# First mixer: the substitution chain of the second pair of heads moved from VectorE to GpSimd

## The chip, the cores and the metric

The kernel runs on one core of a Trainium2 chip. The metric is the device time of one execution in microseconds, as the median of several runs. TensorE is called PE here, VectorE DVE, ScalarE ACT, GpSimd POOL or GpSimd; SP is the engine that issues most DMAs.

## The reference, cut to what matters

The network has a first block (a mixer of windowed attention and an RWKV-7 recurrence, then a gated feed-forward) and a second one of two layers. Sequence 512, width 1024, fp32. The change lies in the recurrence of the first mixer, 8 heads of 64:

```python
def step(state, inp):
    r_t, w_t, k_t, v_t, kk_t, a_t = inp
    sa = jnp.einsum('bhvk,bhk->bhv', state, -kk_t)
    state = (state * w_t[:, :, None, :]
             + sa[..., None] * (kk_t * a_t)[:, :, None, :]
             + v_t[..., None] * k_t[:, :, None, :])
    return state, jnp.einsum('bhvk,bhk->bhv', state, r_t)
```

## The kernel before, in words

Activations are kept with channels on the 128 partitions and the 512 positions along the row. Each dense product with a weight is done as three fp32r matmuls (L243 to L245), from an activation split in two parts (hh, hl) and a weight split in two (wh by ACT at L449, wl by DVE at L450). Weights come by DMA in pieces of 512 KB, through three buffers `raw` (L421, queue of SP).

The recurrence is done in chunks of 64 positions, for a pair of heads j (0 to 3) at a time. Its stages are written in the order that the string `order` in `CFG` gives (L21): D projects r, k and v; A makes decays and the small products within a chunk; I (`inverse_rows`) and J (`inverse_join`) invert a unit lower triangular matrix for each chunk and head; B runs over the eight chunk states. S is windowed attention for a group of heads, Q its query projection. A scheduler then places the instructions of every engine by dependences, priorities and its own estimates of durations, and each engine runs its list in order; the stages I are given a higher priority (L997).

`inverse_rows(j)` works on the two 32 x 32 halves of the diagonal of each 64 x 64 matrix, for 8 chunk-and-head units on the rows:

- L767: ACT fills T (`invt`, one buffer) with the identity; L771: DVE transposes the products `aab` into M (`invm`).
- L773 to L778: forward substitution, 31 steps of two instructions, each a chain link of the last:

```python
        for s in range(31):
            a, t = s // 4 + 1, 31 - s
            tv = tmp[:, :a * t].rearrange("p (a t) -> p a t", t=t)
            E("inv", j).tensor_tensor(tv, T[:, :a, s:s + 1].to_broadcast([P, a, t]),
                                    M[:, s + 1:, s:s + 1].rearrange("p t o -> p o t").to_broadcast([P, a, t]), op=OP.mult)
            E("inv", j).tensor_tensor(T[:, :a, s + 1:], T[:, :a, s + 1:], tv, op=OP.add)
```

- L780: four DMAs write T to DRAM (`s`); L782: GpSimd clears `RT`; L784: four DMAs read it back as diagonal blocks of `RT`.

`E(name, j)` picks the engine from `CFG[name][j]`: V is DVE, G GpSimd, A ACT. `inverse_join(j)` begins with two DVE transposes of RT into `rq` (L798), then matmuls of 32 x 32 (L803, L813). `stage_b(j)` applies RT (L833), adds to the queries (L848) and copies into F (L852), then goes through the states ST: L871 multiplies F with the last state on PE, L875 and L877 add the chunk's own products, L886 makes the next state on DVE (L884 for the first), L888 applies a state to the output. L881 clears the first state of a pair on GpSimd. `swa(j)` has score matmuls L935, softmax pieces L936 to L942, L950 transposes, L959 to L965 the row sums (L963 a reciprocal on DVE, L965 a wide copy of it on GpSimd), L970 values, L974 transposes of that copy, and L919 fetches bias rows by DMAs of GpSimd.

The numbers behind tile names are those of the buffers: `invt_1090`, `invp_1095` (the temporary) and `invm_1089` belong to the second pair, j = 1, `RT_1162` and `rq_1837` to its join; `ST_1304` to `ST_1359` are the states of the first pair.

Of the kernel before, what the change touches and what calls it, by code (L numbers as in the profile page):

```python
# [17 lines left out]
PSUM = bass.MemoryType.PSUM  # L18
DRAM = bass.MemoryType.DRAM

CFG = {'order': 'D0 PK A0 D1 Q0 Q1 I0 A1 I1 J0 B0 Q2 S0 Q3 D2 A2 J1 I2 S1 B1 S2 J2 D3 s0 S3 A3 I3 r1 J3 s2 s1 B2 s3 B3 r0 r2 r3 F', 'inv': 'VVVV', 'rt': 'G', 'bt': 'G', 'bh': 'G', 'kh': 'G', 'kk': 'V', 't1': 'V', 'th': 'G', 'at': 'A', 'ti': 'A', 'sh': 'V', 'bb': 'bbbs', 'ob': 'nnnw', 'fa': 2, 'oa': 2, 'yc': [1, 1], 'xc': [1, 1], 'xa': ['GVGGGGVV', 'GVGGVGGV'], 'ev': 0, 'mb': 'qqb', 'fb': 'qqb', 'rc': 1, 'xm': [('ld', 'cs', 'th', 'dec')], 'xf': [('z', 'z', 'z', 'z')], 'mp': 'on', 'fp': 'os', 'rkv': 5, 'wo0': 0, 'wo1': 0, 'up': 0, 'wi': 0, 'spare': '', 'ahead': 'bno|a', 'hpi': 200, 'uact': 'A'}  # L21

P = 128
S = 512
# [42 lines left out]
class K:  # L67
# [200 lines left out]
    def ffn(self, x, h, up, down, cw, nf, chunks, act, done, bc=None, parts=((0, S),), mid=None, before=None, after=None):  # L268
        nc = self.nc
        if bc is None:  # L270
            self.ahead(up, h, CFG["fa"])
            bc = self.rstd(x)
# [187 lines left out]
def post_add(k, x, y, g, eps, cols, h, g2, i):  # L460
    nc = k.nc
    bc = k.inv_rms(y, eps, chains=CFG["yc"][i])

    def apply():
        for m in range(8):
            yc, xc = y[m], x[m][:, cols[0]:cols[1]]
            nc.vector.scalar_tensor_tensor(yc, yc, k.pv[:, g + m:g + m + 1], bc, op0=OP.mult, op1=OP.mult)
            (nc.vector if CFG["xa"][i][m] == "V" else nc.gpsimd).tensor_tensor(xc, xc, yc, op=OP.add)
            k.scale(x[m], h[m], k.pv[:, g2 + m:g2 + m + 1], cols)
# [4 lines left out]
def boundary(k, x, h, st, applies, banks, tags, post, more=None):  # L474
# [3 lines left out]
    for i, cols in enumerate(HALVES):  # L478
# [3 lines left out]
        if more:  # L482
            more(cols)
        heads.append(k.squares([t[:, c0:c1] for t in x], CFG["xc"][i], tags[i]))
    st.ready += qs
# [12 lines left out]
def first_block(k, I, ctx):  # L498
    with k.phase("m1", dict(M1, rkv=CFG["rkv"])), k.tc.tile_pool(name="ps1", bufs=1, space=PSUM) as k.p1:
        x, h, up, bc = first_mixer(k, I)  # L500
    ps2 = ctx.enter_context(k.tc.tile_pool(name="ps2", bufs=1, space=PSUM))
    k.pairs = [ps2.tile([P, 2, S], F32, name=f"s{i}") for i in range(PAIRS)]
    for m in range(8):
        k.dump(f"x1_{m}", x[m])
    nc = k.nc
    k.c = ctx.enter_context(k.tc.tile_pool(name="cst2", bufs=1))
    with k.phase("f1", F1):
        y, applies, nxt, carry = [], [], [], []

        def done(m, q, acc, cols):  # L510
            nc.vector.tensor_tensor(acc, acc, q, op=OP.add)
            if cols == HALVES[0]:
                y.append([acc])
            else:
                y[m].append(acc)

        def mid():
            rope_tables(k, I, "z")
            carry.append(gate_weights(k, I))

        def before(i):
            if i == 1:
                nxt.append(k.stream(I["ev_w_in"]))
                nxt[1].pool = CFG["ev"]
                nxt[1].prepare(CFG["xf"])

        def after(i, cols):
            if i == 0:
                nxt.append(k.scaled_tiles())
            applies.append(post_add(k, x, [t[i] for t in y], PV["n_ffn_post"], 1e-6, cols, nxt[0], PV["attn_n0"], i))  # L530

        down = k.stream(I["w_ffn_down"])
        k.ffn(x, h, up, down, PV["cw1"], act=AF.Gelu_apprx_tanh, done=done, bc=bc, parts=HALVES, mid=mid, before=before, after=after, **FFN1)
        h, st = nxt
        q = k.pss()
        bc = boundary(k, x, h, st, applies, CFG["fb"], ("zu", "u"), CFG["fp"], lambda cols: gate_dense(k, q, carry[0], h, cols))
    for m in range(8):
        k.dump(f"x2_{m}", x[m])
    return x, h, st, bc, q
# [1336 lines left out]
```

## Time and profile before

| | us |
|---|---|
| median of 3 runs | 2214.72 |
| lowest and highest | 2212.98, 2216.64 |
| profiled execution, its own time | 2216.11 |
| its span in the trace | 2214.4 |

The span is what the views divide; the 1.7 us between it and the execution's own time lie outside the trace. In a timeline each row has the start, the duration, the engine, the line of the kernel, operation, output and inputs without buffer numbers, and in brackets how long the engine sat idle before it and what ended that. [...]

### The profile page before, as it was taken

What the parts mean: (1) busy time and instruction counts of PE and PEld (TensorE: products, weight loads), DVE (VectorE), ACT (ScalarE), POOL (GpSimd) and SP (SyncE); (2) the same over time, 40 slices, a digit from 0 to 9 for tenths busy, and PEclk for the clock granted to TensorE, in tenths of its full rate; (3) what the DMA queues carried; (4) which work ended last, traced back from release to release, by engine and by line L of the source; (5) the groups of instructions that cost most, each with busy time, mean ns of one, the idle gap of its engine ahead of it and who ended that gap; (6) DMA issues with size and microseconds to landing.
All of it is one profiled execution on the core that took longest, in us unless ns stands there. A gap on an engine that the chain in (4) does not pass through costs nothing. (4 is left out here: it accounts for less than half of the span.)

```text
span 2214.4 us, 30032 instructions
## 1 busy us (share of the span) xinstructions
PE 2134.9 (96%) x11732; PEld 1707.0 (77%) x11736; DVE 1388.4 (63%) x2478; ACT 920.7 (42%) x1519; POOL 354.1 (16%) x331
## 2 busy tenths in 40 slices
PE   7899988999999999999999999999999899999998
PEld 6676767888888889976777888888666568888887
DVE  5988856767246666544676653664795656644665
ACT  4345534544234444333444432443334444433443
POOL 2111105111001113201102111111013201111111
PEclk9999998999999999999999999999999999999999
DMA  4210131333323335311112233332211113333334
GB/s 159 72 43 25 54 96 39 91 98 104 98 95 95 99 130 170 110 60 46 57 58 86 95 97 98 100 96 95 68 58 58 38 39 95 96 95 95 98 121 153
DMA packets 66301, 192.81 MB, mean 87 GB/s; under 512 B 15808, under 2 KB 19152, under 8 KB 66160
## 3 DMA queue, kind: packets, MB, share of 16 engines
q1 hardware_dynamic: 65584, 189.70, 27.1%
q0 software_dynamic: 576, 1.19, 0.3%
q8 instruction: 92, 1.51, 0.3%
q14 instruction: 49, 0.40, 0.1%
HBM read 188.24 MB, written 2.63 MB: 86 GB/s over the span
## 5 line engine op out<-in xcount | busy, mean ns | idle before, releaser
L450 DVE TENSOR_TENSOR wl<-raw,wh 128x1024 fp32r<-128x1024 f32 x341 | 431.8, 1267 | 259.9 <-ACT wh L449 259.3
L243 PE MATMUL q<-hh,wh 128*128 128x512 f32 (+1 forms) x1294 | 518.8, 401 | 12.1 <-ACT hh L210 7.7
L449 ACT ACTIVATE wh<-raw 128x1024 fp32r<-128x1024 f32 x341 | 359.8, 1056 | 371.1 <-PE q L244 207.2
L244 PE MATMUL q<-hl,wh 128*128 128x512 f32 (+1 forms) x1294 | 507.2, 392 | 3.8 <-DVE hl L211 3.8
L245 PE MATMUL q<-hh,wl 128*128 128x512 f32 (+1 forms) x1294 | 505.2, 390 | 0.2 <-DVE wl L450 0.2
L243 PEld LDWEIGHTS q<-hh,wh 128*128 128x128 f32 x1294 | 246.4, 191 | 61.8 <-ACT hh L210 7.7
L244 PEld LDWEIGHTS q<-hl,wh 128*128 128x128 f32 x1294 | 246.6, 191 | 53.8 <-issue 6.0
L245 PEld LDWEIGHTS q<-hh,wl 128*128 128x128 f32 x1294 | 246.0, 190 | 52.8 <-issue 2.9
L243 PE MATMUL b<-hh,wh 128*128 128x512 f32 (+1 forms) x602 | 237.5, 394 | 0.0
L244 PE MATMUL b<-hl,wh 128*128 128x512 f32 (+1 forms) x602 | 231.6, 385 | 1.5 <-DVE hl L211 1.5
L245 PE MATMUL b<-hh,wl 128*128 128x512 f32 (+1 forms) x602 | 231.8, 385 | 0.0
L294 POOL TENSOR_TENSOR zu<-za,z 128x512 f32<-128x512 f32 x76 | 100.8, 1327 | 814.6 <-DVE z L289 758.6
L243 PE MATMUL q<-gh,wh 128*128 128x256 f32 (+1 forms) x559 | 189.2, 338 | 2.5 <-ACT wh L449 1.4
L245 PE MATMUL q<-gh,wl 128*128 128x256 f32 (+1 forms) x559 | 188.8, 338 | 1.2 <-DVE wl L450 1.1
L244 PE MATMUL q<-gl,wh 128*128 128x256 f32 (+1 forms) x559 | 187.7, 336 | 0.0
L150 ACT ACTIVATE gh<-zu 128x512 fp32r<-128x512 f32 x76 | 48.1, 632 | 250.5 <-POOL zu L294 250.5
L151 DVE TENSOR_TENSOR gl<-zu,gh 128x512 fp32r<-128x512 f32 x76 | 52.6, 692 | 150.8 <-ACT gh L150 150.8
L183 POOL TENSOR_TENSOR nsq<-nsq,nsq 128x256 f32<-128x256 f32 (+1 forms) x84 | 97.3, 1160 | 253.9 <-ACT nsq L178 253.6
L287 ACT ACTIVATE z<-u,pv 128x512 f32<-128x512 f32 x152 | 122.6, 809 | 31.2 <-DVE u L286 31.2
L244 PEld LDWEIGHTS b<-hl,wh 128*128 128x128 f32 x602 | 114.2, 190 | 24.1 <-DVE hl L211 2.3
L245 PEld LDWEIGHTS b<-hh,wl 128*128 128x128 f32 x602 | 114.0, 189 | 23.4 <-issue 1.0
L243 PEld LDWEIGHTS b<-hh,wh 128*128 128x128 f32 x602 | 114.3, 190 | 22.7 <-issue 2.7
(589 smaller groups left out, 3241.7 us busy)
## 6 DMA issues: line engine op xcount, KB each, us to landing
raw<-in_ffn_up SPq DMA_DIRECT2D x88, 512.0 KB, 3.4
raw<-in_w_ffn_up SPq DMA_DIRECT2D x64, 512.0 KB, 3.4
raw<-in_ffn_down SPq DMA_DIRECT2D x55, 512.0 KB, 3.4
raw<-in_w_ffn_down SPq DMA_DIRECT2D x48, 512.0 KB, 3.4
raw<-in_ev_w_in SPq DMA_DIRECT2D x24, 512.0 KB, 3.5
raw<-in_w_in SPq DMA_DIRECT2D x20, 512.0 KB, 3.5
raw<-in_od_w_in SPq DMA_DIRECT2D x20, 512.0 KB, 3.4
x<-in_x SPq DMA_DIRECT2D x16, 256.0 KB, 3.7
```

The lines of the kernel that those rows point to most:

```text
L150: nc.scalar.activation(hi, x, AF.Copy)
L151: nc.vector.tensor_tensor(lo, x, hi.bitcast(F32), op=OP.subtract)
L183: (nc.gpsimd if m % chains == 0 else nc.vector).tensor_tensor(acc, acc, sq, op=OP.add)
L243: nc.tensor.matmul(o, wh, xh, start=(k == 0), stop=False)
L244: nc.tensor.matmul(o, wh, xl, start=False, stop=False)
L245: nc.tensor.matmul(o, wl, xh, start=False, stop=(k == n - 1))
L287: nc.scalar.activation(y, v, AF.Identity, bias=col(3), scale=col(2))
L294: nc.gpsimd.tensor_tensor(u, a, z[1], op=OP.mult)
L449: nc.scalar.activation(a, part, AF.Copy)
L450: (nc.gpsimd if self.pool > 0 else nc.vector).tensor_tensor(b, part, a.bitcast(F32), op=OP.subtract)
```

## The change

One letter of `CFG` is changed, and with it the engine that the two instructions of a step run on for j = 1:

```diff
-CFG = {'order': '...', 'inv': 'VVVV', ...}
+CFG = {'order': '...', 'inv': 'VGVV', ...}
```

The 62 instructions of the second pair leave DVE's list and enter GpSimd's. The scheduler also places others anew around them. Three places:

GpSimd, between stage A of the second pair (`kk_930`, `th_925`) and the clearing of a first state; the chain's start, the changed order.

```order
L724 TENSOR_TENSOR kk_930<-kti_973,dec_927 128x512
L723 TENSOR_TENSOR th_925<-ksq_931,dec_927 128x512
L776 TENSOR_TENSOR invp_1095<-invt_1090,invm_1089 128x31
L778 TENSOR_TENSOR invt_1090<-invt_1090,invp_1095 128x31
L776 TENSOR_TENSOR invp_1095<-invt_1090,invm_1089 128x30
L778 TENSOR_TENSOR invt_1090<-invt_1090,invp_1095 128x30
```

Before, the second of these rows was followed by L782, the clearing of `RT_1162`; that now stands in the middle of the chain, and L881 (`ST_2143`) and L965 (`sws_1506`) behind its last row.

DVE, in the states of the first pair (ST) and the attention of the first group (es, sws); the order before, at the second pair's join.

```order
L644 TENSOR_TENSOR u_1588<-q_1557,bc_352 128x512
L450 TENSOR_TENSOR wl_1633<-raw_1630,wh_1632 128x1024
L647 SCALAR_TENSOR_TENSOR rkv_1590<-u_1588,pv,rkv_1590 128x511
L798 STREAM_TRANSPOSE rq_1837<-RT_1162 32x256 x2
L910 TENSOR_TENSOR rwo_1395<-rwo_1395,b_1398 128x512
```

And the changed order, where the two transposes stand now:

```order
L886 SCALAR_TENSOR_TENSOR ST_1332<-ST_1323,pc_558,b_1326 128x128
L938 TENSOR_REDUCE es_1441<-sws_1481 128x2
L798 STREAM_TRANSPOSE rq_1837<-RT_1162 32x256
L886 SCALAR_TENSOR_TENSOR ST_1341<-ST_1332,pc_558,b_1335 128x128
L939 TENSOR_TENSOR es_1441<-es_1441,nsink_414 128x2
L1094 SCALAR_TENSOR_TENSOR swq_1555<-q_1524,bc_352 128x512
L450 TENSOR_TENSOR wl_1597<-raw_1594,wh_1596 128x1024
L886 SCALAR_TENSOR_TENSOR ST_1350<-ST_1341,pc_558,b_1344 128x128
L959 TENSOR_TENSOR es_1441<-es_1441,sink_412 128x8
L798 STREAM_TRANSPOSE rq_1837<-RT_1162 32x256
```

The pair of transposes moved up from behind the third pair's first projection into the first pair's states, one ahead of ST_1341 and one behind ST_1350.

SP, the DMAs of the second pair's chain among the loads of w_in; the difference.

```order
 L421 DMA raw_2373<-in_w_in 128x1024
-L421 DMA raw_2409<-in_w_in 128x1024
 L780 DMA s_1_1088<-invt_1090 32x8x32 x4
 L784 DMA RT_1162<-s_1_1088 32x8x32 x4
+L421 DMA raw_2409<-in_w_in 128x1024
 L421 DMA raw_2445<-in_w_in 128x1024
```

One weight load moved behind the eight DMAs of the chain. On ACT, the filling of the third pair's T (L767, `invt_1881`) moved up, ahead of the weight copy `wh_1596` and the exponentials of `sws_1481`. On PE the instructions are the same; ahead of the matmul L871 that reads ST_1341 there are two fewer of the projections `q_1524` and `q_1557`.

## Rows read from the trace of the kernel before

**Rows 1.** The page, busy time of each engine over the whole span

```profile
PE 2134.9 (96%) x11732; PEld 1707.0 (77%) x11736; DVE 1388.4 (63%) x2478; ACT 920.7 (42%) x1519; POOL 354.1 (16%) x331
```

**Rows 2.** Windows around the chain: stretch, us, PE, PEld, DVE, ACT, POOL busy, PEclk

```profile
125.00:130.00 5.00, 5.00 (x63) 4.40 (x63) 4.55 (x20) 3.75 (x12) 0.00 (x0) 1.00 0.00 0
130.00:135.00 5.00, 3.77 (x115) 3.53 (x117) 4.45 (x19) 1.47 (x5) 0.95 (x1) 1.00 0.01 3
135.00:150.00 15.00, 14.87 (x145) 10.98 (x141) 12.63 (x48) 5.89 (x17) 1.57 (x4) 1.00 0.11 37
```

**Rows 3.** Waits of PE, 120 to 170 us: total, times, longest

```profile
PE b L843 <- ACT F L852: 1.2, 1, 1.2
```

**Rows 4.** Timeline of DVE: start, us; chain's transpose, a state step, chain's last

```profile
123.18 1.97 DVE L771 STREAM_TRANSPOSE invm<-aab 128x1024 f32<-128x1024 f32 x1 [0.38 <-ACT aab L770]
...
144.81 0.35 DVE L886 SCALAR_TENSOR_TENSOR ST<-ST,pc,b 128x128 f32<-128x128 f32 x1
...
151.11 0.16 DVE L778 TENSOR_TENSOR invt<-invt,invp 128x8 f32<-128x8 f32 x1
```

**Rows 5.** Timeline of DVE: the join's transposes and a later weight split

```profile
159.04 0.89 DVE L798 STREAM_TRANSPOSE rq<-RT 32x256 f32<-32x256 f32 x2
...
169.52 1.23 DVE L450 TENSOR_TENSOR wl<-raw,wh 128x1024 fp32r<-128x1024 f32 x1 [0.22 <-ACT wh L449]
```

**Rows 6.** Groups of GpSimd by shape, two-input products: busy us, mean ns of one

```profile
L294 POOL TENSOR_TENSOR zu<-za,z 128x512 f32<-128x512 f32 x76 | 100.8, 1327 | 814.6 <-DVE z L289 758.6 <-ACT za L292 50.6 <-DVE strictb L1045 5.4
...
L1567 POOL TENSOR_TENSOR e<-e,sg 128x127 f32<-128x127 f32 x8 | 3.1, 409 | 64.7 <-DVE sg L1566 64.7
```

**Rows 7.** Timeline of DVE, then of GpSimd: a release, and the clearing of RT

```profile
116.35 0.16 DVE L705 TENSOR_SCALAR ar<-kk 128x8 f32<-128x8 f32 x1
...
116.65 1.36 POOL L724 TENSOR_TENSOR kk<-kti,dec 128x512 f32<-128x512 f32 x1 [0.77 <-DVE ar L705]
...
130.11 0.95 POOL L782 MEMSET RT<- 128x1024 f32 x1 [11.08 <-PE b L833]
```

**Rows 8.** Groups of DVE by shape: chain's two operations, a 512-wide product

```profile
L776 DVE TENSOR_TENSOR invp<-invt,invm 128x60 f32<-128x60 f32 x12 | 3.2, 266 | 0.2
...
L714 DVE TENSOR_TENSOR kti<-rkv,ld 128x512 f32<-128x512 f32 x4 | 2.7, 683 | 0.0
...
L778 DVE TENSOR_TENSOR invt<-invt,invp 128x60 f32<-128x60 f32 x12 | 2.6, 217 | 0.2
```

**Rows 9.** Timeline of DVE, the first pair's chain: first, second, twentieth instruction

```profile
82.84 0.21 DVE L776 TENSOR_TENSOR invp<-invt,invm 128x31 f32<-128x31 f32 x1
83.08 0.19 DVE L778 TENSOR_TENSOR invt<-invt,invp 128x31 f32<-128x31 f32 x1
...
87.76 0.23 DVE L778 TENSOR_TENSOR invt<-invt,invp 128x66 f32<-128x66 f32 x1
```

**Rows 10.** Timeline of DVE, the fourth pair's chain: its end, the join's transpose

```profile
291.50 0.18 DVE L778 TENSOR_TENSOR invt<-invt,invp 128x8 f32<-128x8 f32 x1
...
295.72 0.43 DVE L798 STREAM_TRANSPOSE rq<-RT 32x256 f32<-32x256 f32 x1 [0.89 <-DMA RT<-s]
```

**Rows 11.** Timeline of PE: a state step, the transposes of attention

```profile
145.62 0.38 PE L871 MATMUL b<-ST,F 128*128 128x128 f32 x2
...
150.97 0.66 PE L974 MATMUL w<-ident,sws 128*128 128x128 f32 x4
```

**Rows 12.** Windows around two pauses of PE; columns as in rows 2

```profile
104.90:108.20 3.30, 0.01 (x1) 0.01 (x1) 3.30 (x10) 0.37 (x1) 2.42 (x2) 1.00 0.03 12
109.80:113.00 3.20, 3.20 (x8) 1.76 (x7) 2.41 (x4) 1.17 (x2) 0.00 (x0) 0.51 0.22 33
332.80:338.10 5.30, 5.30 (x24) 5.29 (x25) 2.65 (x6) 1.59 (x4) 1.46 (x2) 0.50 0.00 0
```

**Rows 13.** Timeline of SP, then of ACT: weight loads, T's initial copy

```profile
114.20 32.62 SPq L421 DMA_DIRECT2D raw<-in_w_in  x2
...
156.54 0.40 ACT L767 ACTIVATE invt<-tinit 128x256 f32<-128x256 f32 x1
```

More of the change, by code (lines that the diff above doesn't have):

```diff
@@ L19 @@
 DRAM = bass.MemoryType.DRAM
-CFG = {'order': 'D0 PK A0 D1 Q0 Q1 I0 A1 I1 J0 B0 Q2 S0 Q3 D2 A2 J1 I2 S1 B1 S2 J2 D3 s0 S3 A3 I3 r1 J3 s2 s1 B2 s3 B3 r0 r2 r3 F', 'inv': 'VVVV', 'rt': 'G', 'bt': 'G', 'bh': 'G', 'kh': 'G', 'kk': 'V', 't1': 'V', 'th': 'G', 'at': 'A', 'ti': 'A', 'sh': 'V', 'bb': 'bbbs', 'ob': 'nnnw', 'fa': 2, 'oa': 2, 'yc': [1, 1], 'xc': [1, 1], 'xa': ['GVGGGGVV', 'GVGGVGGV'], 'ev': 0, 'mb': 'qqb', 'fb': 'qqb', 'rc': 1, 'xm': [('ld', 'cs', 'th', 'dec')], 'xf': [('z', 'z', 'z', 'z')], 'mp': 'on', 'fp': 'os', 'rkv': 5, 'wo0': 0, 'wo1': 0, 'up': 0, 'wi': 0, 'spare': '', 'ahead': 'bno|a', 'hpi': 200, 'uact': 'A'}
+CFG = {'order': 'D0 PK A0 D1 Q0 Q1 I0 A1 I1 J0 B0 Q2 S0 Q3 D2 A2 J1 I2 S1 B1 S2 J2 D3 s0 S3 A3 I3 r1 J3 s2 s1 B2 s3 B3 r0 r2 r3 F', 'inv': 'VGVV', 'rt': 'G', 'bt': 'G', 'bh': 'G', 'kh': 'G', 'kk': 'V', 't1': 'V', 'th': 'G', 'at': 'A', 'ti': 'A', 'sh': 'V', 'bb': 'bbbs', 'ob': 'nnnw', 'fa': 2, 'oa': 2, 'yc': [1, 1], 'xc': [1, 1], 'xa': ['GVGGGGVV', 'GVGGVGGV'], 'ev': 0, 'mb': 'qqb', 'fb': 'qqb', 'rc': 1, 'xm': [('ld', 'cs', 'th', 'dec')], 'xf': [('z', 'z', 'z', 'z')], 'mp': 'on', 'fp': 'os', 'rkv': 5, 'wo0': 0, 'wo1': 0, 'up': 0, 'wi': 0, 'spare': '', 'ahead': 'bno|a', 'hpi': 200, 'uact': 'A'}
 P = 128
```

## The prediction

> **What bounds the kernel now.** First the page: TensorE (PE) is busy for 2134.9 of 2214.4 us [rows 1], so a change elsewhere counts only where it makes PE wait or ends a wait of PE. Then the windows around the chain that moves. PE is busy 5.00 of 5.00, 3.77 of 5.00 and 14.87 of 15.00 us there, while DVE carries the whole chain beside its other work [rows 2]. PE's list of waits from 120 to 170 us has one entry above 0.3 us: 1.2 us at L843, for ACT's copies into F, which waited for DVE's L848 [rows 3]. Then DVE's own timeline: the chain's source M is ready at 125.15 us (123.18 + 1.97), and its 62nd instruction ends at 151.27 (151.11 + 0.16) [rows 4]. Nothing on PE waits for it. The join, whose two transposes read what the chain leads to, runs at 159.04 [rows 5]. So the chain costs this kernel nearly nothing where it is: it is spread through 26 us in which PE has other work.
>
> **What the change removes.** 62 instructions leave DVE. At most PE gets back the 1.2 us at L843. I book nothing for it, because this wait lies ahead of a new one, told below, and what PE gains before a wait it loses in it. The remaining waits of PE there are shorter still.
>
> **What the chain takes on GpSimd.** The 62 instructions come in a row, each needing the one before. The 31 products (L776) work on 31, 30, 29, 28, 54, ... 16, 8 elements, 1560 in all, and the 31 additions (L778) on as many: 3120. No row shows GpSimd at such sizes; the nearest are its two-input products of 127 elements, 409 ns, and of 512, 1327 ns [rows 6]. A line through both is 918 / 385 = 2.38 ns an element and 106 ns an instruction. That gives 62 x 0.106 + 3120 x 0.00238 = 6.6 + 7.4 = 14.0 us. Between two dependent instructions lies a release. DVE's L705 ended at 116.51 and GpSimd's L724, which waited for it, began at 116.65: 0.14 us, so 62 x 0.14 = 8.7 us. RT's clearing, 0.95 us, stands in the middle of the chain in GpSimd's queue [rows 7]. The products read M with a stride; on DVE such a product takes 266 ns where the addition of the same size takes 217 [rows 8], and I give GpSimd the same 49 ns, 31 x 0.049 = 1.5 us. Sum T = 14.0 + 8.7 + 0.95 + 1.5 = 25.2 us.
>
> The bounds: at least 14.0 us with DVE's own 0.03 us between two instructions (83.05 to 83.08) [rows 9] and RT's clearing for nothing, 14.0 + 1.9 = 15.9 us. At most 62 x (0.409 + 0.14) + 0.95 = 35.0 us, if none is cheaper than the smallest that a row shows. I take 25.2, since the fitted line and the measured release are both rows of GpSimd.
>
> **Who waits for it.** The way back is the fourth pair's: its chain ends at 291.68 (291.50 + 0.18), and the join's first transpose, which sat idle for the DMA into RT, starts at 295.72 [rows 10]: 4.04 us for the way through DRAM. In the changed order this transpose stands on DVE ahead of the step that makes the fifth state, ST_1341, and DVE runs in order. So the chain's end now decides when this step runs: 4.04 + 0.43 (L798) + 0.35 (L886, 0.35 in [rows 4]) = 4.8 us behind it. Behind that DVE has the query's scaling, a weight split and the next state step; PE has, in order, L871 on ST_1341, then projections, attention and the rest. PE cannot pass.
>
> Before, PE began this L871 at 145.62 [rows 11]. The new order has two projection matmuls fewer ahead of it, 0.23 us each by their spacing, so the same point of work is 145.2. Now it can begin at 125.15 + T + 4.8 = 129.95 + T. The shift of everything behind is T - 15.25 us; for T = 25.2, **10.0 us**. The attention transposes L974 at 150.97 [rows 11], whose input GpSimd copies after the chain, do not wait again: that copy needs DVE's reciprocal, itself behind the late state step.
>
> **The clock.** [...] The new pause would be about 10 us, and I add **2.0 us**.
>
> **What costs nothing.** On SP the load of raw_2409 now stands behind the eight DMAs of this chain; it went out near 146.8, at the end of [rows 13]'s two loads, and goes now near 155. Its weights are split at 169.52 [rows 5], which leaves over 10 us; without that cover the cost would be the lateness itself. On ACT, T's refill for the third pair (L767, 0.40 us) moves from 156.54 [rows 13] to ahead of a weight copy, and waits until the chain's DMAs have read T. They are done before the RT transfers that follow them, so ACT is free before DVE is; its backlog up to the next exponentials is about 2 us, and PE first needs those about 1.5 us after it resumes. If that cover fails, it is half a microsecond. GpSimd's later work is now queued behind the chain, whose end I put at 150.4. L965 has to wait for a reciprocal that comes after the late state step anyhow, and the bias rows fetched behind it are first used two projections later. DVE work beside GpSimd's short instructions up to L798 mostly has PSUM as a source, and DVE would wait at L798 anyhow.
>
> **Sum.** 10.0 + 2.0 = 12.0 us. The profiled execution took 2216.11 us (span 2214.4), and would take 2228.1. The median of the runs, 2214.72, is 1.4 lower; against it I predict **2226.7 us**.
>
> **Rivals.**
> First, not slower: GpSimd works through its dependent instructions without the release of 0.14 us and cheaper than the line says, T up to 15.25 us. Then the transpose finds RT there in time, and what remains is up to 1.2 us regained: 2213.5 to 2214.7. The point at which it decides is T = 15.25, 246 ns for each instruction. For it: DVE manages such an instruction in about 0.25 us. Against it: the line alone gives 14.0 us, leaving 1.25 us for 62 releases and RT's clearing. Faster by more than 0.2% would take more than all PE waits of this stretch together.
>
> Second, GpSimd is to DVE at every size what it is at 512 elements: 1327 against 683 ns [rows 6, 8], a ratio of 1.94. DVE's chain by itself, 20 instructions from 82.84 to 87.99 without a break [rows 9], is 0.26 us each, 62 x 0.26 = 16.1 us. Times 1.94 plus 0.95 is T = 32.2, a shift of 17.0 and some 2.3 us for the clock: 2234. For it: both engines have fixed costs an instruction. Against it: at 127 elements the line shows no such fixed cost. [...]
>
> Third, the upper bound: no instruction below 409 + 140 ns, or DVE and GpSimd hinder each other at each one; T = 35.0, a shift of 19.75 and 2.65 for the clock: 2237.1. Nothing in the profile speaks for so high a floor but the lack of a smaller row.
>
> **How the numbers follow.** Forecast (T from 18 to 30, 2219 to 2232) 0.53; ratio 0.22; upper bound 0.10; not slower 0.15. A difference of 0.2%, 4.4 us, is about what a measurement of this kernel can tell from no change. The three slow cases hold 0.85, of which 0.01 falls short of 0.2%; the not-slower case gives 0.11 to no change and 0.04 to faster. So: faster 0.04, same 0.12, slower 0.84. The range must reach into the ends: low 2216, the lower bound T = 15.9 and a little of the clock; high 2238, just past the upper bound. It leaves out the not-slower case, 0.15, and little else.
>
> **What would show it.** In the changed profile: 62 GpSimd rows of L776 and L778 with about 0.4 us from start to start, the last ending near 150; a DVE row L798 with some 10 us of idle before it, released by the DMA into RT; a wait of PE of about that length at L871, released by DVE's L886; a stretch with the clock at 0.5 behind it; the same work later by 12 us from there to the end. It is wrong if the chain ends before 140.4, if L798 finds RT ready, or if PE's wait lies at another line.

## The result, and the profile after

| | us |
|---|---|
| kernel before, median of 4 runs beside the change | 2215.37 |
| changed kernel, median of 4 runs (lowest, highest) | 2228.52 (2226.57, 2230.05) |
| ratio, 95% interval | 1.0062, 1.0048 to 1.0075 |
| profiled execution, its own time; its span | 2228.38; 2226.4 |

The change makes the kernel slower, by 12.0 us in the spans of the two profiled executions (13.2 us by the medians). The medians of later sessions are told with those of the runs of the kernel before that went with them; in each session 4 to 6 of these lie between 2222 and 2227 us, some 10 us above the rest, and pull the ratio that goes with the interval down, so that a slower version looks less slow by the ratio than by the medians, and a faster one faster.

The page's first part. Against [rows 1] DVE lost 62 instructions and 10 us, GpSimd gained 62 and 18 us:

```profile
PE 2136.8 (96%) x11732; PEld 1707.4 (77%) x11736; DVE 1378.2 (62%) x2416; ACT 920.5 (41%) x1519; POOL 372.0 (17%) x393
```

The windows from 140 us on, columns as in [rows 2]; PEclk is the clock granted to PE, 1.00 its full speed. PE does nearly nothing for nine microseconds, and the granted clock stands at 0.50 when it goes on:

```profile
140.00:145.00 5.00, 5.00 (x45) 3.46 (x46) 1.99 (x4) 0.00 (x0) 4.00 (x13) 1.00 0.00 0
145.00:150.00 5.00, 0.56 (x3) 0.12 (x2) 0.00 (x0) 0.00 (x0) 3.50 (x14) 0.88 0.00 0
150.00:155.00 5.00, 0.60 (x2) 0.50 (x2) 1.31 (x5) 2.33 (x5) 0.00 (x0) 0.50 0.31 48
155.00:160.00 5.00, 5.00 (x30) 3.65 (x29) 2.25 (x7) 1.30 (x6) 0.20 (x1) 0.59 0.35 109
```

The list of PE's waits between 100 and 200 us now begins with the step that makes a state; the 1.2 us at L843 [rows 3] are 0.3:

```profile
PE b L871 <- DVE ST L886: 8.8, 1, 8.8
...
PE b L843 <- ACT F L852: 0.3, 1, 0.3
```

GpSimd's timeline: the chain's first three instructions, RT's clearing within it, and the last. From 125.75, when DVE's L771 ends (123.79 + 1.96, against 125.15 in [rows 4]), to 149.53 it takes 23.8 us:

```profile
125.83 0.26 POOL L776 TENSOR_TENSOR invp<-invt,invm 128x31 f32<-128x31 f32 x1 [6.19 <-DVE invm L771]
126.17 0.25 POOL L778 TENSOR_TENSOR invt<-invt,invp 128x31 f32<-128x31 f32 x1
126.50 0.25 POOL L776 TENSOR_TENSOR invp<-invt,invm 128x30 f32<-128x30 f32 x1
...
137.89 0.36 POOL L776 TENSOR_TENSOR invp<-invt,invm 128x75 f32<-128x75 f32 x1
138.18 0.96 POOL L782 MEMSET RT<- 128x1024 f32 x1
139.09 0.34 POOL L778 TENSOR_TENSOR invt<-invt,invp 128x75 f32<-128x75 f32 x1
...
149.32 0.21 POOL L778 TENSOR_TENSOR invt<-invt,invp 128x8 f32<-128x8 f32 x1
```

DVE's timeline. The last row before the gap ends at 143.52; then DVE stands at the join's first transpose until the DMA into RT has landed, and the state step that PE wants comes behind it:

```profile
142.84 0.68 DVE L938 TENSOR_REDUCE es<-sws 128x2 f32<-128x512 f32 x1
153.69 0.43 DVE L798 STREAM_TRANSPOSE rq<-RT 32x256 f32<-32x256 f32 x1 [10.17 <-DMA RT<-s]
154.06 0.29 DVE L886 SCALAR_TENSOR_TENSOR ST<-ST,pc,b 128x128 f32<-128x128 f32 x1
```

ACT's timeline shows a second queue that stands still for the same chain, 13.02 us at the refill of the single buffer T. It is let go when the chain's DMAs have read T, about 1 us before DVE:

```profile
152.66 0.42 ACT L767 ACTIVATE invt<-tinit 128x256 f32<-128x256 f32 x1 [13.02 <-DMA s<-invt]
152.98 1.04 ACT L449 ACTIVATE wh<-raw 128x1024 fp32r<-128x1024 f32 x1
153.93 0.58 ACT L951 ACTIVATE swt<-w 128x512 f32<-128x512 f32 x1
```

PE's timeline at the pause, and attention's transposes of [rows 11] behind it:

```profile
145.16 0.40 PE L243 MATMUL q<-hh,wh 128*128 128x512 f32 x1
154.40 0.79 PE L871 MATMUL b<-ST,F 128*128 128x128 f32 x2 [8.84 <-DVE ST L886]
...
162.43 0.66 PE L974 MATMUL w<-ident,sws 128*128 128x128 f32 x4
```

Where the 12.0 us are: this L871 comes 8.78 us later than in [rows 11] with two projections (0.46 us) still to do, so 9.2 us there, 8.84 of them the wait. L974 comes 11.46 us later; the 2.2 us between the two are the lower clock, 0.50 up to 155 us and 0.59 on average from 155 to 160. 0.5 us more are lost behind it.

One comparison reads against intuition: on DVE the chain ended at 151.27 [rows 4], on GpSimd at 149.53. GpSimd had it done sooner, having nothing but RT's clearing beside it in those 23.8 us. What changed for the worse is where the chain's readers stand.

### The profile page after: what moved, and what is told of

It is laid out like the page before. It is cut to its first block, busy times and chain, and to the rows that moved or that the text cites. A ratio compares the mean times of both kernels' runs of the same rounds, so it can differ in the third digit from the quotient of the medians.

```text
span 2226.4 us, 30038 instructions
## 1 busy us (share of the span) xinstructions
PE 2136.8 (96%) x11732; PEld 1707.4 (77%) x11736; DVE 1378.2 (62%) x2416; ACT 920.5 (41%) x1519; POOL 372.0 (17%) x393
```

## The experiments

The theory: two in-order queues, DVE's at L798 and ACT's at L767, were given the chain's readers ahead of work for PE, and either alone would hold PE nearly as long; the chain on GpSimd costs nothing by itself. The rivals are told with the runs.

**DVE's readers moved back.** The transposes are tied to a value that exists only after the third pair's first projection:

```diff
-        Rc = k.slot("rq", (P, 8, 32))
+        Rc = k.slot("rq", (P, 8, 32)); j == 1 and nc.vector.tensor_copy(Rc[:, 0, 0:1], DP[2][0][:, 0:1])
```

> The changed kernel with one thing undone: DVE's two join transposes of the second pair (L798) are tied to a value of the third pair's first projection, so that they stand on DVE behind L647 and L910, some 20 us later than in the changed kernel, where they stood before the change. The chain stays on GpSimd. Theory A, two queues wait side by side (DVE at L798, ACT at the refill of T, L767, single buffer): DVE's wait is gone, PE passes L871 near 145.5 us, but ACT still stands at L767 until about 152.7, then does a weight copy and two exponentials, so that PE waits at L950 from about 148 to 155.5; with the lower clock behind it about 2225 us (2222 to 2228). Theory B, only DVE's transpose holds PE: no wait above 1.5 us is left, 2214 to 2217. Theory C, the loss comes from GpSimd itself (its later queue, its traffic beside DVE, SP's delayed weight load): about 2228, PE's wait at another line than L871 and L950.

Measured: 2225.05 us against 2215.64 (ratio 1.0038, 1.0025 to 1.0051). PE's waits from 95 to 175 us, and ACT's timeline:

```profile
PE w L950 <- ACT swt L951: 7.4, 1, 7.4
```

```profile
152.50 0.42 ACT L767 ACTIVATE invt<-tinit 128x256 f32<-128x256 f32 x1 [13.02 <-DMA s<-invt]
...
154.75 0.57 ACT L951 ACTIVATE swt<-w 128x512 f32<-128x512 f32 x1
```

DVE's wait is gone and PE is held at another line, by ACT, from 148.0 to 155.4. That is theory A, in the line and the length of the wait; theories B and C fall.

**ACT's reader set free.** The second pair gets its own T:

```diff
-        M, T = k.slot("invm", (P, 32, 32)), k.slot("invt", (P, 8, 32))
+        M, T = k.slot("invm", (P, 32, 32)), k.slot("invu" if j == 1 else "invt", (P, 8, 32))
```

> The changed kernel with one thing undone: the second pair has a buffer of its own for T, so that ACT's refill of T for the third pair (L767) no longer waits for the second chain's DMAs. DVE's transposes stay where the change put them. Theory A and theory B: DVE's L798 still waits about 10 us, PE's wait at L871 stays at 8.5 to 9 us, ACT has no wait above 4 us; 2226 to 2229 us. Theory D, ACT's wait is what holds PE and DVE's only ends at the same time: PE's wait shrinks to under 3 us, below 2220.

Measured: 2227.45 us against 2215.64 (ratio 1.0039, 1.0024 to 1.0055). PE's waits, and ACT's longest:

```profile
PE b L871 <- DVE ST L886: 8.9, 1, 8.9
```

```profile
154.97 0.51 ACT L942 ACTIVATE sws<-sws,es 128x256 f32<-128x256 f32 x1 [8.80 <-DVE es L939]
```

PE's wait is as it was, and D falls. One point of the expectation was wrong: ACT does wait above 4 us, 8.80 us, now for DVE's L939, which stands behind L798 too.

**Both.** The two edits together.

> Both edits together, chain on GpSimd. Theory A: neither queue stands behind the chain any more; PE has no wait above 1.5 us between 120 and 170 us and keeps the full clock there; 2213 to 2216 us, the time of the kernel before. The chain itself still takes 23 to 25 us on GpSimd. Theory C (GpSimd's own later work, SP's weight load behind the chain's DMAs, or traffic of GpSimd beside DVE is part of the loss): between 2218 and 2228 us, with a wait of PE at a line behind these.

Measured: 2215.78 us against 2215.64 (ratio 0.9996, 0.9983 to 1.0008). The first rows of PE's waits from 95 to 175 us, and the windows in which PE stood still in the changed kernel:

```profile
PE o L718 <- DVE invt L778: 3.3, 1, 3.3
PE o L691 <- ACT ld L675: 0.8, 1, 0.8
```

```profile
145.00:150.00 5.00, 5.00 (x40) 3.25 (x39) 3.28 (x7) 1.00 (x3) 4.28 (x13) 1.00 0.00 1
150.00:155.00 5.00, 4.90 (x26) 3.69 (x22) 3.86 (x16) 1.32 (x3) 0.88 (x2) 1.00 0.52 95
```

The whole loss is gone, with the chain on GpSimd as in the changed kernel (124.29 to 149.11, 24.8 us). GpSimd's later work, SP's late weight load and traffic beside DVE cost nothing that a run can tell: theory C falls.

**The same edits on the kernel before.**

> Control: the kernel before, chain on DVE, with the same two edits (a buffer of its own for the second pair's T, the transposes tied behind the third pair's first projection). Theory A: the edits by themselves are worth nothing, 2213.5 to 2216.5 us, PE's 1.2 us at L843 is still there. If it comes out faster than that, the edits are worth something of their own, and the run with both edits on the changed kernel has to be read against this one.

Measured: 2215.38 us against 2215.64 (ratio 1.0002, 0.9985 to 1.0018), and of PE's waits:

```profile
PE b L843 <- ACT F L852: 1.2, 1, 1.2
```

The edits are worth nothing by themselves. The sources of these two kernels differ by the engine of the chain alone, 2215.78 and 2215.38 us: that move, with what the scheduler rearranges for it, is worth nothing that a run can tell.

**The same cure without the buffer.** Instead of a second T, the third pair's refill is tied like the transposes, so that L767 stands later on ACT:

```diff
-        M, T = k.slot("invm", (P, 32, 32)), k.slot("invt", (P, 8, 32))
+        M, T = k.slot("invm", (P, 32, 32)), k.slot("invt", (P, 8, 32)); j == 2 and nc.vector.tensor_copy(T[:, 0, 0:1], DP[2][0][:, 0:1])
```

> The changed kernel, chain of the second pair on GpSimd, no buffer added: the two join transposes and the third pair's refill of T (L767) are both tied to the third pair's first projection, so that neither DVE nor ACT has anything that needs the chain ahead of work for PE. Theory A: same as with the extra buffer, no wait of PE above 1.5 us between 120 and 170 us, 2213 to 2217 us. If the extra buffer mattered for more than the place of L767, it is slower than that.

Measured: 2215.28 us against 2215.84 (ratio 0.9988, 0.9972 to 1.0003). A second T is not needed: moving the readers out of the way cures the loss.

**The first pair's chain instead.** PE's largest wait here, 3.3 us at L718, is released by DVE, which works through the first chain at that time. `'inv': 'GVVV'`, both edits above, and the first pair's transposes tied:

```diff
+        Rc = k.slot("rq", (P, 8, 32)); j < 1 and nc.vector.tensor_copy(Rc[:, 0, 0:1], R[1]["ar"][:, 0, 0, 0:1])
```

> The first pair's chain on GpSimd instead of the second's (the second's back on DVE), with its join transposes tied behind L705 of the second pair's preparation, the third pair's refill of T tied to the third pair's first projection, and a buffer of its own for the second pair's T. In the kernel before, PE waits 3.3 us at L718 near 105 us while DVE works through the first chain beside the second pair's preparation, and loses about 1.6 us to the lower clock behind it. Theory A (a chain on GpSimd costs nothing where no in-order queue stands behind it): PE's wait at L718 shrinks below 1.5 us, 2209.5 to 2213 us. Rival: GpSimd's own L706 and L710, which stand behind the chain in its queue, come several us later and PE waits for them instead near 112 to 118 us; 2214 to 2219 us.

Measured: 2219.68 us against 2215.84 (ratio 1.0012, 1.0000 to 1.0025). The expected gain missed, and the rival came, 0.7 us above its range. The wait at L718 is down to 0.4 us, but of PE's waits:

```profile
PE a L740 <- DVE rq L795: 4.6, 1, 4.6
...
PE o L718 <- DVE t L716: 0.4, 1, 0.4
```

L795 is the copy that ties the transposes. It stands right behind DVE's L713, and that one waited for GpSimd's L712:

```profile
115.11 0.69 DVE L713 TENSOR_TENSOR ksq<-ksq,ld 128x512 f32<-128x512 f32 x1 [4.84 <-POOL ksq L712]
```

GpSimd's timeline shows the cause, the chain's last instruction and what had to queue behind it, and the windows show what the pause did to the clock:

```profile
111.84 0.21 POOL L778 TENSOR_TENSOR invt<-invt,invp 128x8 f32<-128x8 f32 x1
112.01 0.62 POOL L710 TENSOR_SCALAR th<-th 128x512 f32<-128x512 f32 x1
112.59 1.26 POOL L706 TENSOR_TENSOR ar<-rkv,dec 128x512 f32<-128x512 f32 x1
113.81 1.26 POOL L712 TENSOR_TENSOR ksq<-kk,th 128x512 f32<-128x512 f32 x1
```

```profile
115.00:120.00 5.00, 4.14 (x65) 3.75 (x66) 4.05 (x13) 0.34 (x1) 2.65 (x3) 0.61 0.59 149
120.00:125.00 5.00, 5.00 (x67) 3.96 (x67) 3.12 (x9) 0.73 (x3) 0.00 (x0) 0.50 0.58 194
125.00:140.00 15.00, 14.62 (x213) 12.46 (x213) 11.94 (x41) 9.35 (x30) 0.95 (x1) 0.84 0.01 2
```

**Both pairs' chains.** `'inv': 'GGVV'` with the edits of that run.

> The first and the second pair's chains on GpSimd, each with the edits that keep its readers off the queues (join transposes tied, refill of T tied, a buffer of its own for the second pair's T). Theory A: the gain of the first pair's move, and most of the 1.2 us at L843 besides; 2208.5 to 2212.5 us. Rival as in the run with the first pair alone, 2214 to 2219 us.

Measured: 2222.73 us against 2215.84 (ratio 1.0021, 1.0007 to 1.0035), a wait of 5.0 us at L740: the rival's mechanism again, 3.7 us above its range.

**The queue behind the first chain cleared.** The second pair's L706, L710 and L712 go to DVE (`E("rt", j)`, `E("th", j)`, `E("bt", j)` with `'GVGG'`), and the first pair's transposes are tied behind the second pair's last L744:

```diff
+        Rc = k.slot("rq", (P, 8, 32)); j < 1 and nc.vector.tensor_copy(Rc[:, 0, 0:1], R[1]["aab"][:, 7, 0:1])
```

> As the run with the first pair's chain on GpSimd, with what held it mended: the second pair's preparation (L706, L710, L712) runs on DVE instead of behind the chain in GpSimd's queue, and the first pair's join transposes are tied behind the second pair's last L744, so that DVE doesn't stand at the chain's DMAs ahead of L744. Theory A: PE's 4.6 us at L740 shrink to 1 to 2.5 us and the long stretch at half clock behind it to at most 3 us; 2211 to 2215 us. Rival: DVE, with 1.9 us more of its own, becomes the bound ahead of L740, PE waits 3 us and more there and the clock falls as before; 2215 to 2220 us.

Measured: 2212.46 us against 2214.54 (ratio 0.9980, 0.9967 to 0.9992). The largest wait of PE from 80 to 175 us is 1.0 us, and the clock holds:

```profile
PE o L718 <- DVE pc L726: 1.0, 1, 1.0
```

```profile
110.00:115.00 5.00, 5.00 (x50) 3.42 (x50) 5.00 (x12) 1.12 (x2) 4.37 (x10) 1.00 0.00 0
115.00:120.00 5.00, 4.78 (x51) 3.78 (x51) 4.52 (x12) 2.90 (x9) 1.66 (x2) 1.00 0.31 47
```

**The second pair's chain on GpSimd as well.**

> The same, and the second pair's chain on GpSimd too with its readers tied. Theory A: like the run with the first pair alone, less most of the 1.2 us at L843 of the kernel before; 2210 to 2214.5 us. Rival: as there, 2215 to 2220 us.

Measured: 2214.03 us against 2214.54 (ratio 0.9988, 0.9973 to 1.0003, without one run of 2382.24 us), within the expectation, but not better than with the first chain alone. GpSimd's L965 now stands behind the second chain, and PE waits for it:

```profile
PE w L974 <- POOL sws L965: 0.9, 1, 0.9
```

**A control of that gain, and the run once more.** The same edits with all chains on DVE:

> Control for the run with the first pair's chain on GpSimd and the second pair's preparation on DVE: the same edits, all chains on DVE. Theory A (what that run gained came from taking the first chain off DVE, not from the edits around it): DVE has the first chain and 1.9 us more of its own beside it, PE's 3.3 us at L718 are back or longer, 2214.5 to 2219 us. Rival (the edits around it, L706, L710 and L712 no longer going through GpSimd, are what gained): no more than 2213 us.

> The run with the first pair's chain on GpSimd and the second pair's preparation on DVE, once more on the same chip as its control, so that the two are compared with the same runs of the kernel before: 2211 to 2214 us again.

Measured on one chip against 2215.76 us: the control 2219.94 us, with widely scattered runs (2215.33 to 2227.62 us, and one of 5357.76 that the ratio leaves out; ratio 1.0013, 0.9997 to 1.0029), the version with the first chain on GpSimd 2212.86 us (ratio 0.9980, 0.9966 to 0.9993). So, over the whole kernel, the edits gain nothing without the move. Edits and move together gain 2.1 and 2.9 us on the kernel before, by the medians of the two runs, some 0.1% (0.2% by the ratios).

The control, 0.9 us above theory A's range, doesn't bear out that theory's reason, though. The expected 3.3 us at the second pair's L718 did not come back: 0.31 us are left there, with the chain on DVE. DVE is done with L716 at 107.56 instead of 108.08 us, and PE comes to L718 later, with five more projections ahead of it and a mean clock of 0.83 from 100 to 110 us, where the kernel before has 0.98. From the first pair's L718 to the third pair's L771 the kernel before takes 126.85 us (64.07 to 190.92), the control 125.27 (63.87 to 189.14), and the version with the first chain on GpSimd 123.69 (64.61 to 188.30): in this stretch the edits alone gain about half of what edits and move gain together. The control's profiled execution loses it again further on and ends 1.1 us behind the kernel before; why stays open.

## Why the prediction was right

The forecast was 2226.7 us; the median is 2228.52, within its range of 2216 to 2238. The mechanism is the one that was forecast: L798 sat idle for the DMA into RT, PE waited at L871 for the late L886, the chain ended near 150 us, and none of the three signs of being wrong came. Step by step:

- **T, the chain on GpSimd: 23.8 us, predicted 25.2.** Two terms were mis-sized, in opposite directions, so that the closeness of T is in part luck. By the groups of GpSimd's lines between 120 and 150 us the 31 products took 9.4 us and the 31 additions 8.8, together 18.2 where line and stride gave 15.5: the line through 127 and 512 elements is too cheap below them (8 elements 0.20 us, the line says 0.125). RT's clearing cost 0.8 us (137.89 to 139.09 from one start to the next, where 0.40 is usual). What is left, 4.8 us, is 0.08 us for each of 62 releases, where I took 0.14 from a release between two engines [rows 7]. The products, which read M with the stride, took 19 ns more than the additions (302 against 283), not 49.
- **The way back: 4.16 us, predicted 4.04** (149.53 to 153.69). The last two steps took 0.71 us up to PE's L871 where 0.78 was booked.
- **The shift: 8.84 us of waiting, predicted 10.0.** L871 began at 154.40, forecast 155.15, and PE was ready for it at 145.56, forecast 145.2; in the prediction's own terms, from 145.2, the shift is 9.2 us. That the second pair's source came 0.6 us later has nothing to do with the change: PE's wait ahead of it at L740 is 0.9 us here and 0.2 before, but it is also 0.9 us in the kernel before with both edits, and 0.3 in the changed kernel with both.
- **The clock: 2.2 us, predicted 2.0.** No run shows the term of 2.0 us, nor the 2.3 and 2.65 us of the rivals; they were the author's estimates. What is shown is work at 0.51 and at 0.50 elsewhere [rows 12], and in the changed kernel some 4.7 us of work at 0.50 behind this pause, half of which is 2.35. The shortfall of the shift and the 0.5 us lost later nearly cancel; 12.0 us of sum and 12.0 us of difference agree better than the terms do.
- **L843's 1.2 us** did shrink to 0.3, and were lost in the wait behind, as booked.
- **ACT's refill booked at nothing** because "ACT is free before DVE is": right in the number (ACT was free at 152.66, DVE at 153.69), but the margin was 1.0 us. The experiments show what the sum couldn't: it is a full second cause. Taking DVE's wait away alone leaves 7.4 us on PE.
- **SP and GpSimd booked at nothing:** right. With both readers moved, the weight load and L965 stand behind the chain as in the change, and the time is that of the kernel before.
- **The rivals.** T up to 15.25 us fell. The ratio of 1.94 fell at these sizes: at 60 elements GpSimd took 0.33 and 0.31 us (timeline at 141.13 and 141.53) where DVE takes 0.266 and 0.217 [rows 8], 1.24 and 1.43 times as long. The upper bound fell with the release of 0.08.

Why the scheduler set L798 and L767 so early was not tested.

## What to carry to other kernels

Moving a dependent chain to an idle engine moves its readers too: look in the new order at every in-order queue that now stands in front of the chain's end, and ask what PE needs from behind that place. Cure all such queues together, since undoing one of two parallel waits shows almost nothing (2225 and 2227 us with one undone, 2215.8 with both). Then look at what is queued behind the chain on its new engine: with the first pair's chain there, PE's wait of 4.6 us came from that queue, and clearing it, together with a later place for the transposes, brought 2219.7 down to 2212.5 us (in two sessions; the two edits were not tried apart).

## What the runs showed of the hardware

In several places of these runs a short instruction of GpSimd or DVE takes 1.15 to 1.29 us and ends just behind a long one of the other engine. In the run with both edits the chain has one product of 35 elements that takes 1.21 us where the neighbours take 0.3. In GpSimd's timeline, and in DVE's:

```profile
144.67 0.27 POOL L778 TENSOR_TENSOR invu<-invu,invp 128x42 f32<-128x42 f32 x1
145.02 1.21 POOL L776 TENSOR_TENSOR invp<-invu,invm 128x35 f32<-128x35 f32 x1
146.31 0.25 POOL L778 TENSOR_TENSOR invu<-invu,invp 128x35 f32<-128x35 f32 x1
```

```profile
144.88 1.21 DVE L450 TENSOR_TENSOR wl<-raw,wh 128x1024 fp32r<-128x1024 f32 x1
```

It ends at 146.23, just behind DVE's weight split, which has two inputs in SBUF and ends at 146.09. Beside DVE's work with an input in PSUM, such as L936, no chain instruction of the changed kernel is longer: L936 runs there from 141.82 to 142.51, and the product of 66 elements at 141.92 takes 0.34 us, as the one at 132.20 does with DVE idle. In the first pair's run, where DVE does three such splits and part of the second pair's preparation meanwhile, one chain instruction beside each split takes 1.15, 1.29 and 1.20 us and ends 0.14 to 0.19 us behind it, and the chain takes 29.0 us (83.04 to 112.05); in the changed kernel, where DVE had no such work, 23.8, with RT's clearing within it, which the 29.0 do not contain.

It goes the other way too. In the kernel before, an addition of 24 elements of the first chain, on DVE, ends at 106.14, behind a GpSimd product of 512 elements that ends at 106.09; the additions of 24 elements in the third and the fourth chain, at 218.90 and 289.58 with GpSimd idle, take 0.18 us. In DVE's timeline before, and in GpSimd's:

```profile
104.86 1.28 DVE L778 TENSOR_TENSOR invt<-invt,invp 128x24 f32<-128x24 f32 x1
```

```profile
104.83 1.26 POOL L706 TENSOR_TENSOR ar<-rkv,dec 128x512 f32<-128x512 f32 x1 [27.31 <-ACT dec L684]
```

In these runs the stretch at the lower clock doesn't follow the pause's length. By the windows' clocks PE worked some 4.7 us at 0.50 behind the pause of 8.8 us (0.6 us up to 155 and 5 x 0.41 / 0.5 in the window at 0.59); the clock had already fallen within this pause (1.00 up to 148 us, 0.50 from 149). Behind the pause of 4.6 us in the first pair's run it stood at 1.00 up to 115 us, 0.9 us before PE was at work again, and some 13.7 us of work at 0.50 followed (5 x 0.39 / 0.5, 5.0 and 15 x 0.16 / 0.5), where products of 64 and 32 rows (L740, L741, L803) came next in place of the 512-wide projections. In the control with the second pair's preparation on DVE the mean clock from 100 to 110 us was 0.83, with PE busy for 9.69 of these 10 us, behind a wait of 0.8 us at L691; behind the same wait, 0.77 us, it kept 1.00 from 99.5 to 105 us in the kernel before.
